# Seven block products instead of eight in the second MLP product of a hybrid decoder layer

## The chip, the cores and the metric

The kernel runs on one core of one Trainium2 chip, as one launch. The metric is device time in microseconds (us); the kernel before takes 1138.74 us (median of 3 runs, 1137.78 to 1138.87). TensorE (PE) multiplies matrices; PEld is its weight load, which overlaps the products. VectorE (DVE), ScalarE (ACT) and GpSimd (POOL) do element-wise work, and SyncE's queue (SP) issues nearly all DMAs.

## The reference

One layer (DEPTH = 1) over T = 272 tokens (16 learned meta tokens ahead of 256), width 2048, all in float32:

```
h = h + rmsnorm(mix, g_post_mix[l])
hn = rmsnorm(h, g_pre_ffn[l])
ff = jnp.square(jax.nn.relu(hn @ mlp_w1[l])) @ mlp_w2[l]
h = h + rmsnorm(ff, g_post_ffn[l])
return h[:, N_META:]
```

`mix` is the product of four mixers (S5, mLSTM, FoX attention, pooling) with `w_out`. `mlp_w1` is 2048 x 8192 and `mlp_w2` is 8192 x 2048. The change lies in the last product, of a 256 x 8192 activation with `mlp_w2` (the kernel works on the 256 tokens that are returned).

## The kernel before, in words

Every large weight is streamed from memory once, in jobs of 1 MB: a stage tile `wst` of 128 x 2048 (3 buffers) is loaded by one DMA. A job has two halves of 128 x 1024. `do_split` makes of each half two tiles in the PE's fp32r format: `wh` is a rounded copy (ACT, line 138), `wl` the rest, `wst - wh` (DVE, line 139). A product of two fp32 operands is then three fp32r products: high x high, high x low and low x high. The tiles `wh` and `wl` have 4 buffers each. The activations are split the same way by `split_act`: `ah` (ACT, line 173) and `al` (DVE, line 174), 128 x 256 for each channel tile, 4 buffers.

`stream` goes over all halves: before the products of half i are issued, the splits up to half i + 3 (`LOOK`) and the loads of the next two jobs have been issued. The order in which the instructions of one engine then stand is chosen by a planner, which works through the program by priority and by what its model finds ready; each engine runs its own queue strictly in that order.

The first MLP product (`up`, lines 1172 and 1173) leaves its result, channels on the partitions, in `H` and `Y`: 64 channel tiles of 128 channels x 256 tokens. The second product is two calls of `row_jobs` (line 223), one for each 1024 of the 2048 output columns. A job holds two channel tiles, a pair, of `mlp_w2`; there are 32 pairs in a call and 64 in all. For each channel tile, 2 token tiles of 128 and 2 column blocks of 512 make 4 accumulators of 128 x 512, each in a PSUM bank (tags `a0` to `a3` in the first call, `m0` to `m3` in the second), with three matmuls each: 24 matmuls of 128x128 by 128x512 for a pair. The last 2 (first call) or 4 (second call) channel tiles are held back and run accumulator by accumulator, so that `evac_a` and `evac_b` (square sums on ACT, line 1192; gain on DVE, lines 1201 and 1212; the residual and the output at the end, lines 1219 to 1223) can start on the first accumulators while PE works on the others.

`XC` (128 x 16 x 2 x 272 in fp32r) holds the split input of the first product and is not read any more once that is done.

Of the kernel before, what the change touches and what calls it, by code (L numbers as in the profile page):

```python
# [29 lines left out]
TH = T // 2  # L33
NK = D // P
DFF = 8192
NF = DFF // P
# [9 lines left out]
TILES = ((0, 16), (16, 128), (144, 128))  # L46
LOOK = 3
PACE = 2.0


def build(tc, A, out):
# [10 lines left out]
class Body:  # L62
# [41 lines left out]
    def need(self, *names):  # L104
        while not all(n in self.ready for n in names):
            yield 0
# [13 lines left out]
    def stream(self):  # L120
        nc = self.nc
        jobs = self.jobs
        halves = [(j, h) for j in jobs for h in range(2)]
        split = {}

        def do_split(i):
            j, h = halves[i]
            src = j["stage"][:, h * 1024:(h + 1) * 1024]
            if j.get("early"):
                wh = self.sb(self.post, [P, 1024], f"wh{j['early']}{h}", F32R)  # L130
                wl = self.sb(self.post, [P, 1024], f"wl{j['early']}{h}", F32R)
            else:
                wh = self.sb(self.wsp, [P, 1024], "wh", F32R)
                wl = self.sb(self.wsp, [P, 1024], "wl", F32R)
            n = 512 if i == 0 else 1024
            for a in range(0, 1024, n):
                cs = slice(a, a + n)
                nc.scalar.copy(wh[:, cs], src[:, cs])  # L138
                nc.vector.tensor_tensor(out=wl[:, cs], in0=src[:, cs], in1=wh[:, cs].bitcast(F32), op=ALU.subtract)  # L139
            split[i] = (wh, wl)  # L140
            if j.get("pre"):
                j["pre"](h)

        done = 0
        early = [i for i, (j, h) in enumerate(halves) if j.get("early")]
        for i, (j, h) in enumerate(halves):
            self.load(i // 2 + 3)
            if i == early[0] - 2:
                self.load(early[-1] // 2 + 1)
            while done < i + LOOK + 1 and done < len(halves) and (done not in early or i >= early[0] - 2):  # L150
                with ExitStack() as es:
                    if early[-1] < done <= early[-1] + LOOK + 1:
                        for ins in self.after:
                            es.enter_context(self.tc.issue_after(ins))
                    do_split(done)
# [12 lines left out]
    def split_act(self, src):  # L168

        nc = self.nc  # L170
        ah = self.sb(self.asp, [P, S], "ah", F32R, bufs=4)
        al = self.sb(self.asp, [P, S], "al", F32R, bufs=4)
        nc.scalar.copy(ah, src)  # L173
        nc.vector.tensor_tensor(out=al, in0=src, in1=ah.bitcast(F32), op=ALU.subtract)
        return ah, al


    def seg_jobs(self, name, w, c0, nk, xh, xl, t0, nt, evac, tags):
# [29 lines left out]
    def row_jobs(self, w, nk, act, need, c0, tags, lead, evac):  # L208

        nc = self.nc
        acc = {}
        sp = {}
        held = []

        def one(tok, c, k, w2):
            if (tok, c) not in acc:  # L220
                acc[tok, c] = self.bank(tags[2 * tok + c])
            for a, b in ((0, 0), (0, 1), (1, 0)):
                ins = nc.tensor.matmul(acc[tok, c], sp[k][a][:, tok * P:(tok + 1) * P], w2[b][:, c * 512:(c + 1) * 512],  # L223
                                       start=(k == 0 and (a, b) == (0, 0)), stop=(k == nk - 1 and (a, b) == (1, 0)))
            return ins.ins

        def job(k0):
            def pre(h):
                k = k0 + h
                if need:  # L230
                    self.drain(need(k))
                sp[k] = self.split_act(act(k))

            def mm(h, wh, wl):
                k = k0 + h
                if k < nk - lead:
                    for tok in range(2):
                        for c in range(2):
                            one(tok, c, k, (wh, wl))
                    return  # L240
                held.append((k, (wh, wl)))
                if k == nk - 1:
                    last = None
                    for tok in range(2):
                        for c in range(2):
                            with self.tc.issue_after(last) if last else nullcontext():
                                for kk, ww in held:
                                    ins = one(tok, c, kk, ww)
                            last = ins
                            with self.tc.high_priority():  # L250
                                evac(tok, c, acc[tok, c])
            return {"src": w[:, k0:k0 + 2, c0:c0 + 1024], "a": 2, "pre": pre, "mm": mm}

        return [job(k0) for k0 in range(0, nk, 2)]

    def rstd(self, ss, n, width, rows=P):

# [805 lines left out]
    def out_jobs(self):  # L1063
        nc, A = self.nc, self.A
        w = A["w_out"].rearrange("(k p) c -> p k c", p=P)
        act = lambda k: self.Y[:, k, :]
        st = {}

        def square(tok, c, acc):
# [82 lines left out]
    def ffn_jobs(self):  # L1152
# [1 line left out]
        w1 = A["mlp_w1"].rearrange("(k p) c -> p k c", p=P)  # L1154
        w2 = A["mlp_w2"].rearrange("(k p) c -> p k c", p=P)

        act = lambda f: self.H[:, f, :] if f < NF - NK else self.Y[:, f - (NF - NK), :]

        def up(g):
            tags = [f"{'ma'[g % 2]}{b}" for b in range(4)]  # L1160
            state = {}

            def mm_for(k0):
                def mm(h, wh, wl):
                    for b in range(4):
                        if b not in state:
                            state[b] = self.bank(tags[b])
                        acc = state[b]
                        for kk in range(2):
                            k = k0 + 2 * h + kk  # L1170
                            ws = slice(kk * 512 + b * P, kk * 512 + (b + 1) * P)
                            nc.tensor.matmul(acc.rearrange("p (a b) -> p a b", a=2), wh[:, ws], XC[:, k, :, 0:S], start=(k == 0), stop=False)  # L1172
                            nc.tensor.matmul(acc[:, 0:S], wl[:, ws], XC[:, k, 0, 0:S], start=False, stop=(k == NK - 1))  # L1173
                        if k0 + 2 * h + 2 == NK:
                            lo = z = self.sb(self.fp, [P, S], "lo", bufs=3)
                            nc.scalar.copy(lo, acc[:, S:2 * S])
                            nc.vector.tensor_tensor(out=z, in0=acc[:, 0:S], in1=lo, op=ALU.add)
                            nc.vector.scalar_tensor_tensor(out=z, in0=z, scalar=0.0, in1=self.rb2, op0=ALU.max, op1=ALU.mult)
                            nc.scalar.activation(act(4 * g + b), z, AF.Square)
                return mm  # L1180

# [7 lines left out]
        st = {}  # L1189
# [4 lines left out]
        def evac_a(tok, c, acc):  # L1194
            if (tok, c) == (0, 0):
                st["ss"] = self.sb(self.fp, [P, 2, 5], "fss")
                nc.gpsimd.memset(st["ss"][:, :, 4:5], EPS)
                st["m"] = self.sb(self.fp, [P, 2, 2, 512], "fm")
                st["gp"] = self.gain(self.fp, "g_post_ffn", 0)
            square(tok, c, acc)  # L1200
            nc.vector.tensor_tensor(out=st["m"][:, tok, c, :], in0=acc, in1=st["gp"][:, c * 512:(c + 1) * 512], op=ALU.mult)
            if (tok, c) == (1, 1):
                st["gp"] = self.gain(self.fp, "g_post_ffn", 1)

        def evac_b(tok, c, acc):
            X = self.X
            square(tok, 2 + c, acc)
            if c == 1:
                r = self.sb(self.fp, [P, 1], f"fr{tok}")
                self.rms(r, st["ss"][:, tok, :])  # L1210
            f = st[c] = self.sb(self.fp, [P, 512], "fin", bufs=2)
            nc.vector.tensor_tensor(out=f, in0=acc, in1=st["gp"][:, c * 512:(c + 1) * 512], op=ALU.mult)
            if c == 0:
                return
# [7 lines left out]
                    nc.vector.scalar_tensor_tensor(out=X[:, tok, cs], in0=m, scalar=r, in1=X[:, tok, cs], op0=ALU.mult, op1=ALU.add)  # L1222
                (nc.scalar if cc == 0 else nc.sync).dma_start(self.out[tok * P:(tok + 1) * P, cs], X[:, tok, cs])

        jobs += self.row_jobs(w2, NF, act, None, 0, ["a0", "a1", "a2", "a3"], 2, evac_a)
        jobs += self.row_jobs(w2, NF, act, None, 1024, ["m0", "m1", "m2", "m3"], 4, evac_b)
        return jobs


# [24 lines left out]
```

## Time and profile before

| | |
|---|---|
| median of 3 runs | 1138.74 us |
| time of the profiled execution | 1138.89 us |
| its span | 1136.9 us |
| PE busy | 1109.5 us (98%) |
| DVE busy | 717.2 us (63%) |
| ACT busy | 570.0 us (50%) |
| POOL busy | 196.1 us (17%) |
| mean DMA rate | 179 GB/s |

Busy time is the time in which at least one instruction of the engine was running. An instruction's duration in the profile can include a wait inside it, for instance for a port; its start can lie a little ahead of the end of the one before it on the same engine. Matmuls are pipelined: one of 128x512 shows 0.39 us, and the next starts well before that is over, so the pace is read from a stretch and its count. The second MLP product runs from about 780 us to 1128 us.

### The profile page before, as it was taken

The page shows a single profiled execution, that of the slowest core. Times are in us where ns is not written, and L with a number is a line of the kernel's source. Part 1 is how long each engine was busy: PE and PEld are TensorE (multiplying, and loading weights), DVE is VectorE, ACT ScalarE, POOL GpSimd, SP SyncE. Part 2 cuts the span into 40 slices and gives each one's busy share as a digit, 9 for nine tenths or more (in the row PEclk, how much of TensorE's full clock was granted, in tenths as well). Part 3 has the DMA queues.
Part 4 walks back from the last instruction along what each step waited for, and adds up shares of the span by engine and source line. Part 5 has one row for each costly group of instructions (what it writes and reads, how often), then busy time and mean ns, then how long its engine had stood idle before and what let it go on. Part 6 is the DMA issues. An engine that isn't in the chain of part 4 may idle for free.

```text
span 1136.9 us, 16603 instructions
## 1 busy us (share of the span) xinstructions
PE 1109.5 (98%) x6425; PEld 959.8 (84%) x6425; DVE 717.2 (63%) x1042; ACT 570.0 (50%) x918; POOL 196.1 (17%) x266
## 2 busy tenths in 40 slices
PE   8998999999999999999999999999999999999996
PEld 7897887999988878888888888888888888888885
DVE  5589998545556676555555555655666666666565
ACT  5634335445645567455445444545545455454543
POOL 6948887002151010000000000000000000000001
PEclk9999999999999999999999999999999999999999
DMA  8734334535447655665656566665655666556652
GB/s 252 214 96 155 112 112 137 175 126 175 152 131 261 214 172 179 199 191 186 190 186 185 186 185 189 186 191 172 222 190 185 192 202 217 186 189 197 203 189 74
DMA packets 91822, 203.31 MB, mean 179 GB/s; under 512 B 12996, under 2 KB 16192, under 8 KB 91488
## 3 DMA queue, kind: packets, MB, share of 16 engines
q1 hardware_dynamic: 90800, 201.45, 55.4%
q8 instruction: 50, 0.82, 0.3%
q10 hardware_dynamic: 848, 0.79, 0.2%
q14 instruction: 28, 0.23, 0.1%
q0 software_dynamic: 96, 0.02, 0.0%
HBM read 199.58 MB, written 2.11 MB: 177 GB/s over the span
## 4 chain that ended last, share of the span: by engine, by line
PE 83%; DVE 6%; POOL 3%; issue 1%; SPq 0%; ACT 0%; DMA 0%; DVEq 0%; POOLq 0%; ACTq 0%
PE a L223 19%; PE m L223 19%; PE m L1172 10%; PE a L1172 10%; PE m L1173 5%; PE a L1173 5%; PE a L197 3%; PE a L196 3%; PE a L195 3%; DVE wl L139 2%; DVE cv L864 1%; POOL si L836 1%; DVE wr L824 0%; POOL sr L834 0%; SPq L775 0%
## 5 line engine op out<-in xcount | busy, mean ns | idle before, releaser
L139 DVE TENSOR_TENSOR wl<-wst,wh 128x1024 fp32r<-128x1024 f32 (+1 forms) x365 | 454.9, 1248 | 271.9 <-ACT wh L138 271.6
L138 ACT CAST wh<-wst 128x1024 fp32r<-128x1024 f32 (+1 forms) x365 | 380.9, 1046 | 253.1 <-PE a L1172 85.3
L1172 PE MATMUL m<-xc,wh 128*128 128x512 f32 x512 | 179.9, 394 | 0.1
L1172 PE MATMUL a<-xc,wh 128*128 128x512 f32 x512 | 179.4, 394 | 0.0
L195 PE MATMUL a<-xc,wh 128*128 128x272 f32 (+2 forms) x576 | 168.3, 296 | 0.9 <-ACT wh L138 0.9
L196 PE MATMUL a<-xc,wh 128*128 128x272 f32 (+2 forms) x576 | 167.8, 293 | 0.0
L197 PE MATMUL a<-xc,wl 128*128 128x272 f32 (+2 forms) x576 | 166.9, 293 | 0.0
L1173 PE MATMUL m<-xc,wl 128*128 128x256 f32 x512 | 143.4, 280 | 0.0
L1173 PE MATMUL a<-xc,wl 128*128 128x256 f32 x512 | 143.0, 280 | 0.0
L223 PE MATMUL m<-wl,ah 128*128 128x512 f32 x320 | 124.6, 389 | 0.2 <-DVE wl L139 0.2
L223 PE MATMUL a<-wl,ah 128*128 128x512 f32 x320 | 124.7, 390 | 0.0
L223 PE MATMUL a<-wh,al 128*128 128x512 f32 x320 | 124.7, 390 | 0.0
L223 PE MATMUL m<-wh,al 128*128 128x512 f32 x320 | 124.5, 389 | 0.0
L223 PE MATMUL m<-wh,ah 128*128 128x512 f32 x320 | 123.2, 389 | 0.0
L223 PE MATMUL a<-wh,ah 128*128 128x512 f32 x320 | 123.1, 391 | 0.0
L367 POOL TENSOR_TENSOR fr<-fr,mhalf 128x1 f32<-128x1 f32 x2 | 1.1, 558 | 688.6 <-DVE fr L366 688.6
L1172 PEld LDWEIGHTS m<-xc,wh 128*128 128x128 f32 x512 | 96.1, 188 | 23.0 <-DVE xc L1132 0.3
L1172 PEld LDWEIGHTS a<-xc,wh 128*128 128x128 f32 x512 | 96.0, 188 | 22.8
L195 PEld LDWEIGHTS a<-xc,wh 128*128 128x128 f32 x576 | 109.3, 191 | 3.6 <-ACT wh L138 1.3
L196 PEld LDWEIGHTS a<-xc,wh 128*128 128x128 f32 x576 | 110.3, 192 | 1.4 <-issue 0.4
L197 PEld LDWEIGHTS a<-xc,wl 128*128 128x128 f32 x576 | 109.4, 191 | 1.7 <-issue 0.9
L173 ACT CAST ah<-h 128x256 fp32r<-128x256 f32 x96 | 38.9, 407 | 118.8 <-PE a L223 60.3
(310 smaller groups left out, 1442.7 us busy)
## 6 DMA issues: line engine op xcount, KB each, us to landing
wst<-in_mlp_w SPq DMA_DIRECT2D x128, 1024.0 KB, 5.2
wst<-in_w_in SPq DMA_DIRECT2D x34, 1024.0 KB, 5.1
wst<-in_w_out SPq DMA_DIRECT2D x16, 1024.0 KB, 5.2
x<-in_x SPq DMA_DIRECT2D x8, 256.0 KB, 3.5
wst<-in_ssm_glu_w SPq DMA_DIRECT2D x2, 1024.0 KB, 5.0
res<-in_x SPq DMA_DIRECT2D x1, 2048.0 KB
wst<-in_w_in SPq DMA_DIRECT2D x3, 512.0 KB, 8.5
out<-res SPq DMA_DIRECT2D x6, 256.0 KB, 2.4
```

Of the source, the lines that this page charges most:

```text
L138: nc.scalar.copy(wh[:, cs], src[:, cs])
L139: nc.vector.tensor_tensor(out=wl[:, cs], in0=src[:, cs], in1=wh[:, cs].bitcast(F32), op=ALU.subtract)
L173: nc.scalar.copy(ah, src)
L195: nc.tensor.matmul(acc[:, :nt], sh, xh(k, t0, nt), start=(k == 0), stop=False)
L196: nc.tensor.matmul(acc[:, :nt], sh, xl(k, t0, nt), start=False, stop=False)
L197: nc.tensor.matmul(acc[:, :nt], sl, xh(k, t0, nt), start=False, stop=(k == nk - 1))
L223: ins = nc.tensor.matmul(acc[tok, c], sp[k][a][:, tok * P:(tok + 1) * P], w2[b][:, c * 512:(c + 1) * 512], start=(k == 0 and (a, b) == (0, ...
L367: nc.gpsimd.tensor_tensor(out=dst, in0=dst, in1=self.mhalf[:, :dst.shape[1]], op=ALU.pow)
L836: g.tensor_tensor(out=si, in0=wr[:, ps], in1=sin[:, ps], op=ALU.mult)
L864: v.scalar_tensor_tensor(out=c, in0=x(tap), scalar=w(tap), in1=c, op0=ALU.mult, op1=ALU.add)
L1172: nc.tensor.matmul(acc.rearrange("p (a b) -> p a b", a=2), wh[:, ws], XC[:, k, :, 0:S], start=(k == 0), stop=False)
L1173: nc.tensor.matmul(acc[:, 0:S], wl[:, ws], XC[:, k, 0, 0:S], start=False, stop=(k == NK - 1))
```

## The change

29 of the 64 pairs go another way. `KINDS` says which: in the first call two plain pairs (N) and then 15 times S, N; in the second two plain ones, 14 times S, N, and two plain ones. A plain pair is computed as before (`plain`). For an S pair, the two channel tiles, the two token tiles and the two column blocks are taken as a 2 x 2 block product in Winograd's form of Strassen's: 7 block products of sums (`seven`), each three matmuls, 21 in all. The sums are made by POOL: four 128 x 512 differences of weight blocks, in place in the stage tile, and four 128 x 128 sums of activation blocks (tile `sums`). ACT and DVE split the plain weight blocks B11, B22 and B21 (1536 columns, into `whR`, `wlR`) ahead of the differences, and after them the four differences (2048 columns, into `whT`, `wlT`) and the four activation sums (512 columns, into `ahS`, `alS`). All these are single buffers, cut from `XC`. Four of the products (M1, M5, M6, M7) have accumulators of their own in the four PSUM banks that the call does not use; after the call's last S pair they are combined into four SBUF tiles (one ACT copy, four DVE adds), and at the end each plain accumulator gets its part added (one more DVE instruction) before `evac_a` or `evac_b`.

`split_act` now splits a pair's activations at once (128 x 512, 2 buffers instead of 4 of 128 x 256), with the second half of a job; `row_jobs`, which the product with `w_out` still uses, does so too. The tile `lo` of the first product has 2 buffers instead of 3, and `fin` is gone.

```diff
+KINDS = ("NN" + "SN" * 15, "NN" + "SN" * 14 + "NN")
...
         def do_split(i):
             j, h = halves[i]
+            if j.get("split"):
+                split[i] = j["split"](h, j["stage"])
+                return
...
-        ah = self.sb(self.asp, [P, S], "ah", F32R, bufs=4)
-        al = self.sb(self.asp, [P, S], "al", F32R, bufs=4)
+        ah = self.sb(self.asp, [P, 2 * S], "ah", F32R, bufs=2)
+        al = self.sb(self.asp, [P, 2 * S], "al", F32R, bufs=2)
...
+        whR, wlR, whT, wlT = cut(0, 1536), cut(1536, 1536), cut(3072, 2048), cut(5120, 2048)
+        ahS, alS = cut(7168, 512), cut(7680, 512)
...
+        def three(dst, ah, al, wh, wl, stop):
...
+            nc.tensor.matmul(b, ah, wh, start=first, stop=False)
+            nc.tensor.matmul(b, ah, wl, start=False, stop=False)
+            return nc.tensor.matmul(b, al, wh, start=False, stop=stop).ins
...
+                            with self.tc.high_priority():
+                                v = acc["part"][2 * tok + c]
+                                nc.vector.tensor_tensor(out=v, in0=acc[tok, c], in1=v, op=ALU.add)
+                                evac(tok, c, v)
...
+            def split(h, st):
+                b12, b11, b22, b21 = (st[:, i * 512:(i + 1) * 512] for i in range(4))
+                def hl(wh, wl, src):
+                    nc.scalar.copy(wh, src)
+                    nc.vector.tensor_tensor(out=wl, in0=src, in1=wh.bitcast(F32), op=ALU.subtract)
+                sub = lambda eng, o, a, b: eng.tensor_tensor(out=o, in0=a, in1=b, op=ALU.subtract)
+                if h == 0:
+                    hl(whR[:, 0:512], wlR[:, 0:512], b11)
+                    hl(whR[:, 512:1536], wlR[:, 512:1536], st[:, 1024:2048])
+                    return None, None
+
+                sub(nc.gpsimd, b11, b12, b11)
+                sub(nc.gpsimd, b12, b12, b22)
+                sub(nc.gpsimd, b22, b22, b11)
+                sub(nc.gpsimd, b21, b21, b22)
+                a = act(k0)
+                a11, a21, a12, a22 = (a[:, i * P:(i + 1) * P] for i in range(4))
+                sums = self.sb(self.fp, [P, 512], "sums")
+                s3, s2, s1, s4 = (sums[:, i * P:(i + 1) * P] for i in range(4))
+                sp[k0], sp[k0 + 1] = self.split_act(a)
+                sub(nc.gpsimd, s3, a21, a11)
+                nc.gpsimd.tensor_tensor(out=s1, in0=a21, in1=a22, op=ALU.add)
+                sub(nc.gpsimd, s2, s1, a11)
+                sub(nc.gpsimd, s4, a12, s2)
+                hl(ahS, alS, sums)
+                hl(whT[:, 0:1024], wlT[:, 0:1024], st[:, 0:1024])
+                hl(whT[:, 1024:2048], wlT[:, 1024:2048], st[:, 1024:2048])
+                return None, None
...
+                todo = ((("M1", "A11", "B11"), ((0, 1), "A12", "B21"), ((0, 0), "S4", "B22")),
+                        (("M5", "S1", "T1"), ("M7", "S3", "T3"), ("M6", "S2", "T2"), ((1, 1), "A22", "T4")))[h]
+                for dst, x, y in todo:
+                    three(dst, *A[x], *B[y], final and dst[0] == "M")
+                if h == 1 and final:
+                    add = lambda o, a, b: nc.vector.tensor_tensor(out=o, in0=a, in1=b, op=ALU.add)
+                    with self.tc.high_priority():
+                        c12, c11, c22, c21 = acc["part"] = part()
+                        nc.scalar.copy(c11, acc["M1"])
+                        add(c21, acc["M6"], c11)
+                        add(c12, acc["M5"], c21)
+                        add(c21, acc["M7"], c21)
+                        add(c22, acc["M5"], c21)
...
-                            lo = z = self.sb(self.fp, [P, S], "lo", bufs=3)
+                            lo = z = self.sb(self.fp, [P, S], "lo", bufs=2)
...
-        jobs += self.row_jobs(w2, NF, act, None, 0, ["a0", "a1", "a2", "a3"], 2, evac_a)
-        jobs += self.row_jobs(w2, NF, act, None, 1024, ["m0", "m1", "m2", "m3"], 4, evac_b)
+        ta, tm = ["a0", "a1", "a2", "a3"], ["m0", "m1", "m2", "m3"]
+        jobs += self.fast_jobs(w2, NF, act2, 0, tm, ta, KINDS[0], 2, part_a, evac_a)
+        jobs += self.fast_jobs(w2, NF, act2, 1024, ta, tm, KINDS[1], 4, part_b, evac_b)
```

## Rows read from the trace of the kernel before

**Rows 1.** Engines by busy time (share of the span), instructions: the page's first part.
```profile
PE 1109.5 (98%) x6425; PEld 959.8 (84%) x6425; DVE 717.2 (63%) x1042; ACT 570.0 (50%) x918; POOL 196.1 (17%) x266
```

**Rows 2.** Busy time by stretch: us, engines (instructions), granted clock, DMA share, GB/s.
```profile
780.00:953.00 173.00, 173.00 (x765) 143.24 (x764) 105.85 (x133) 88.06 (x135) 0.00 (x0) 1.00 0.59 191
954.00:1117.00 163.00, 163.00 (x721) 134.97 (x720) 100.79 (x123) 82.76 (x124) 0.00 (x0) 1.00 0.58 187
```

**Rows 3.** Last part of the chain that ended last: start, us, what.
```profile
779.60 174.19 PE a L223 x768
953.79 162.99 PE m L223 x719
```

**Rows 4.** Waits in 780 to 1117 us: waiter and releaser, total us, times, longest.
```profile
ACT ah L173 <- PE a L223: 82.1, 59, 4.3
ACT ah L173 <- PE m L223: 80.2, 59, 1.4
```

**Rows 5.** ACT and DVE groups by shape, 780 to 1117 us: busy, mean ns.
```profile
L138 ACT CAST wh<-wst 128x1024 fp32r<-128x1024 f32 x124 | 129.8, 1046 | 0.2 <-PE a L1172 0.2
L173 ACT CAST ah<-h 128x256 fp32r<-128x256 f32 x92 | 37.4, 407 | 118.8 <-PE a L223 60.3 <-PE m L223 58.5
...
L139 DVE TENSOR_TENSOR wl<-wst,wh 128x1024 fp32r<-128x1024 f32 x124 | 151.9, 1225 | 61.0 <-ACT wh L138 61.0
L174 DVE TENSOR_TENSOR al<-h,ah 128x256 fp32r<-128x256 f32 x92 | 39.1, 425 | 50.1 <-ACT ah L173 50.0
```

**Rows 6.** The split's two lines, whole span: min/median/max ns (the 128x512 form is the shortest).
```profile
L138 ACT CAST wh<-wst x365: 618/1048/1062, 7.0 to 1117.1; 128x1024 fp32r<-128x1024 f32 x182, 128x512 fp32r<-128x512 f32 x1
L139 DVE TENSOR_TENSOR wl<-wst,wh x365: 685/1226/2387, 7.7 to 1118.2; 128x1024 fp32r<-128x1024 f32 x182, 128x512 fp32r<-128x512 f32 x1
```

**Rows 7.** POOL tensor_tensor of 128x512 (mean) and of 128x128 (min/median/max).
```profile
L974 POOL TENSOR_TENSOR keyrow<-keyrow,trimask 128x512 f32<-128x512 f32 x2 | 2.6, 1294 | 2.7 <-DMA keyrow<-grows 2.7
L836 POOL TENSOR_TENSOR si<-wr,sin x16: 446/526/1446, 101.0 to 183.8; 128x128 f32<-128x128 f32 x16
```

**Rows 8.** POOL and DVE side by side at 84 to 89 us: start, us, instruction.
```profile
84.70 1.55 POOL L754 TENSOR_TENSOR sin<-sin,cos 128x544 f32<-128x544 f32 x1
86.21 2.08 POOL L753 TENSOR_TENSOR cos<-tok,s5col 128x544 f32<-128x544 f32 x1
...
84.96 2.38 DVE L139 TENSOR_TENSOR wl<-wst,wh 128x1024 fp32r<-128x1024 f32 x1
```

**Rows 9.** The same at 1130 to 1133 us, 128x512 on both engines.
```profile
1130.68 0.74 DVE L1222 SCALAR_TENSOR_TENSOR res<-fin,fr,res 128x512 f32<-128x512 f32 x1
...
1130.81 1.74 POOL L1220 TENSOR_TENSOR res<-res,fm 128x512 f32<-128x512 f32 x1 [0.83 <-ACT fm L1219]
...
1131.34 1.75 DVE L1222 SCALAR_TENSOR_TENSOR res<-fin,fr,res 128x512 f32<-128x512 f32 x1
```

**Rows 10.** The same at 107 to 111 us, 128x128 on POOL.
```profile
107.11 1.41 DVE L139 TENSOR_TENSOR wl<-wst,wh 128x1024 fp32r<-128x1024 f32 x1
109.51 1.36 DVE L139 TENSOR_TENSOR wl<-wst,wh 128x1024 fp32r<-128x1024 f32 x1
...
107.40 1.44 POOL L836 TENSOR_TENSOR si<-wr,sin 128x128 f32<-128x128 f32 x1
109.87 1.32 POOL L833 TENSOR_TENSOR pm<-wi,sin 128x128 f32<-128x128 f32 x1
```

**Rows 11.** Busy time by stretch (columns as in rows 2) about an early pause of PE.
```profile
93.00:96.60 3.60, 0.12 (x2) 0.00 (x0) 3.60 (x7) 0.66 (x1) 3.60 (x3) 1.00 0.67 258
97.70:101.10 3.40, 3.40 (x18) 3.40 (x18) 3.40 (x7) 3.40 (x7) 1.61 (x3) 0.50 0.00 1
```

**Rows 12.** DVE's gain on a last accumulator, from PSUM, in the kernel's tail.
```profile
1129.27 0.68 DVE L1212 TENSOR_TENSOR fin<-m,gp 128x512 f32<-128x512 f32 x1
```

**Rows 13.** DMA of the MLP weights: issues, KB each, median us to landing.
```profile
wst<-in_mlp_w SPq DMA_DIRECT2D x128, 1024.0 KB, 5.2
```

More of the change, by code (lines that the diff above doesn't have):

```diff
@@ L170, in split_act @@
         nc = self.nc
-        ah = self.sb(self.asp, [P, S], "ah", F32R, bufs=4)
-        al = self.sb(self.asp, [P, S], "al", F32R, bufs=4)
+        ah = self.sb(self.asp, [P, 2 * S], "ah", F32R, bufs=2)
+        al = self.sb(self.asp, [P, 2 * S], "al", F32R, bufs=2)
         nc.scalar.copy(ah, src)
         nc.vector.tensor_tensor(out=al, in0=src, in1=ah.bitcast(F32), op=ALU.subtract)
-        return ah, al
+        return [tuple(t[:, i * S:(i + 1) * S] for t in (ah, al)) for i in range(2)]
     def seg_jobs(self, name, w, c0, nk, xh, xl, t0, nt, evac, tags):
@@ L228, in pre @@
             def pre(h):
-                k = k0 + h
+                if h == 0:
+                    return
                 if need:
-                    self.drain(need(k))
-                sp[k] = self.split_act(act(k))
+                    self.drain(need(k0), need(k0 + 1))
+                sp[k0], sp[k0 + 1] = self.split_act(act(k0))
             def mm(h, wh, wl):
@@ L254, in row_jobs, with fast_jobs, one, plain @@
         return [job(k0) for k0 in range(0, nk, 2)]
+    def fast_jobs(self, w, nk, act, c0, tags, tags7, kinds, lead, part, evac):
+        nc = self.nc
+        free = self.XC.rearrange("p a b c -> p (a b c)")
+        cut = lambda a, n: free[:, a:a + n]
+        whR, wlR, whT, wlT = cut(0, 1536), cut(1536, 1536), cut(3072, 2048), cut(5120, 2048)
+        ahS, alS = cut(7168, 512), cut(7680, 512)
+        acc = {}
+        sp = {}
+        held = []
+        last_s = max(i for i, kd in enumerate(kinds) if kd == "S")
+        tagof = {(t, c): tags[2 * t + c] for t in range(2) for c in range(2)}
+        tagof.update({f"M{m}": tags7[i] for i, m in enumerate((1, 5, 6, 7))})
+        def three(dst, ah, al, wh, wl, stop):
+            first = dst not in acc
+            if first:
+                acc[dst] = self.bank(tagof[dst])
+            b = acc[dst]
+            nc.tensor.matmul(b, ah, wh, start=first, stop=False)
+            nc.tensor.matmul(b, ah, wl, start=False, stop=False)
+            return nc.tensor.matmul(b, al, wh, start=False, stop=stop).ins
+        def one(tok, c, k, w2):
+            ah, al = sp[k]
+            ts, cs = slice(tok * P, (tok + 1) * P), slice(c * 512, (c + 1) * 512)
+            return three((tok, c), ah[:, ts], al[:, ts], w2[0][:, cs], w2[1][:, cs], k == nk - 1)
+        def plain(k0):
+            def pre(h):
+                if h == 1:
+                    sp[k0], sp[k0 + 1] = self.split_act(act(k0))
+            def mm(h, wh, wl):
+                k = k0 + h
+                if k < nk - lead:
+                    for tok in range(2):
+                        for c in range(2):
+                            one(tok, c, k, (wh, wl))
+                    return
+                held.append((k, (wh, wl)))
+                if k == nk - 1:
+                    last = None
+                    for tok in range(2):
+                        for c in range(2):
+                            with self.tc.issue_after(last) if last else nullcontext():
+                                for kk, ww in held:
+                                    ins = one(tok, c, kk, ww)
+                            last = ins
+                            with self.tc.high_priority():
+                                v = acc["part"][2 * tok + c]
+                                nc.vector.tensor_tensor(out=v, in0=acc[tok, c], in1=v, op=ALU.add)
+                                evac(tok, c, v)
+            return pre, mm
+        def seven(k0, final):
+            def split(h, st):
[4 more added lines that the diff above has]
+                sub = lambda eng, o, a, b: eng.tensor_tensor(out=o, in0=a, in1=b, op=ALU.subtract)
+                if h == 0:
+                    hl(whR[:, 0:512], wlR[:, 0:512], b11)
[18 more added lines that the diff above has]
+                return None, None
+            def mm(h, wh, wl):
+                A = {}
+                for kk, (n0, n1) in enumerate((("A11", "A21"), ("A12", "A22"))):
+                    for i, n in enumerate((n0, n1)):
+                        A[n] = tuple(t[:, i * P:(i + 1) * P] for t in sp[k0 + kk])
+                for i, n in enumerate(("S3", "S2", "S1", "S4")):
+                    A[n] = tuple(t[:, i * P:(i + 1) * P] for t in (ahS, alS))
+                B = {n: (whR[:, i * 512:(i + 1) * 512], wlR[:, i * 512:(i + 1) * 512]) for i, n in enumerate(("B11", "B22", "B21"))}
+                B.update({n: (whT[:, i * 512:(i + 1) * 512], wlT[:, i * 512:(i + 1) * 512]) for i, n in enumerate(("T3", "T1", "T2", "T4"))})
+                todo = ((("M1", "A11", "B11"), ((0, 1), "A12", "B21"), ((0, 0), "S4", "B22")),
[11 more added lines that the diff above has]
+                        add(c22, acc["M5"], c21)
+            return split, mm
+        jobs = []
+        for i, kd in enumerate(kinds):
+            j = {"src": w[:, 2 * i:2 * i + 2, c0:c0 + 1024], "a": 2}
+            if kd == "S":
+                j["split"], j["mm"] = seven(2 * i, i == last_s)
+            else:
+                j["pre"], j["mm"] = plain(2 * i)
+            jobs.append(j)
+        return jobs
@@ L1065, in out_jobs @@
         w = A["w_out"].rearrange("(k p) c -> p k c", p=P)
-        act = lambda k: self.Y[:, k, :]
+        act = lambda k: self.Y[:, k:k + 2, :].rearrange("p a b -> p (a b)")
         st = {}
@@ L1155, in ffn_jobs, with act @@
         w2 = A["mlp_w2"].rearrange("(k p) c -> p k c", p=P)
-        act = lambda f: self.H[:, f, :] if f < NF - NK else self.Y[:, f - (NF - NK), :]
+        def act(f, n=1):
+            t, f = (self.H, f) if f < NF - NK else (self.Y, f - (NF - NK))
+            return t[:, f:f + n, :].rearrange("p a b -> p (a b)")
+        act2 = lambda f: act(f, 2)
         def up(g):
@@ L1197, in evac_a @@
                 nc.gpsimd.memset(st["ss"][:, :, 4:5], EPS)
-                st["m"] = self.sb(self.fp, [P, 2, 2, 512], "fm")
                 st["gp"] = self.gain(self.fp, "g_post_ffn", 0)
             square(tok, c, acc)
-            nc.vector.tensor_tensor(out=st["m"][:, tok, c, :], in0=acc, in1=st["gp"][:, c * 512:(c + 1) * 512], op=ALU.mult)
+            nc.vector.tensor_tensor(out=acc, in0=acc, in1=st["gp"][:, c * 512:(c + 1) * 512], op=ALU.mult)
             if (tok, c) == (1, 1):
@@ L1210, in evac_b @@
                 self.rms(r, st["ss"][:, tok, :])
-            f = st[c] = self.sb(self.fp, [P, 512], "fin", bufs=2)
+            f = st[c] = acc
             nc.vector.tensor_tensor(out=f, in0=acc, in1=st["gp"][:, c * 512:(c + 1) * 512], op=ALU.mult)
@@ L1223, in evac_b, with part_a, part_b @@
                 (nc.scalar if cc == 0 else nc.sync).dma_start(self.out[tok * P:(tok + 1) * P, cs], X[:, tok, cs])
-        jobs += self.row_jobs(w2, NF, act, None, 0, ["a0", "a1", "a2", "a3"], 2, evac_a)
-        jobs += self.row_jobs(w2, NF, act, None, 1024, ["m0", "m1", "m2", "m3"], 4, evac_b)
+        def part_a():
+            st["m"] = self.sb(self.fp, [P, 2, 2, 512], "fm")
+            return [st["m"][:, tok, c, :] for tok in range(2) for c in range(2)]
+        def part_b():
+            return [self.H[:, 2 * i:2 * i + 2, :].rearrange("p a b -> p (a b)") for i in range(4)]
+        ta, tm = ["a0", "a1", "a2", "a3"], ["m0", "m1", "m2", "m3"]
+        jobs += self.fast_jobs(w2, NF, act2, 0, tm, ta, KINDS[0], 2, part_a, evac_a)
+        jobs += self.fast_jobs(w2, NF, act2, 1024, ta, tm, KINDS[1], 4, part_b, evac_b)
         return jobs
```

## The prediction

> **What bounds the kernel now.** I read the engines' shares first: PE is busy for 98% of the span, DVE for 63%, ACT for 50%, POOL for 17% [rows 1]. Shares of the whole say little about one stage, so the next view is the busy time by stretch. In the second MLP product (780 to 1117 us) PE is busy in all of 173 and 163 us, DVE in 61% of them, POOL in none; the granted clock is 1.00, the upper of its two levels, 2.4 GHz [rows 2]. The chain that ended last agrees: from 779.60 us on it is one piece of PE for 174.19 us and 768 matmuls [rows 3], so a matmul goes by every 174.19 / 768 = 0.2268 us, though each shows a longer time. A pair of 24 takes 5.44 us, two pairs 10.89 us. The waits say the same from the other side: ACT waits for PE (82.1 and 80.2 us, for the buffers of `ah`), not PE for ACT or DVE [rows 4]. In this stage the time is PE's count of matmuls, and DVE, ACT and the DMA (5.2 us for a job [rows 13], with others in flight) keep up with it.
>
> **What it takes off PE.** An S pair has 21 matmuls instead of 24: 3 x 0.2268 = 0.68 us, for 29 pairs 19.7 us. That is the whole gain, and it comes only if the other engines prepare an S pair and the N pair behind it within PE's new time for both, 45 x 0.2268 = 10.21 us. So I work out one such period, S and N.
>
> **What it adds on ACT.** Casts: for S 512 + 1024 (plain blocks), 512 (activations), 512 (sums), 2 x 1024 (differences); for N 2 x 1024 and 512. With 1.05 us for 1024 [rows 5] and 0.62 us for 512 [rows 6], 5 x 1.05 + 4 x 0.62 = 7.73 us. That fits in 10.21.
>
> **What it adds on DVE and POOL.** DVE subtracts once for each cast. Taken singly, at 1.23 us for 1024 [rows 5] and 0.69 us for 512 [rows 6], 5 x 1.23 + 4 x 0.69 = 8.91 us: it would fit. POOL's four differences of 128x512 at 1.29 us and four sums of 128x128 at 0.45 us [rows 7] are 6.96 us: that fits too. But before, POOL stood still in this stage [rows 2], and the earlier stages show what the two do to each other. At 84.96 us DVE starts a `wl` while POOL runs until 84.70 + 1.55 = 86.25 us; it ends at 87.34 us, 1.09 us after POOL, and takes 2.38 us instead of 1.23. POOL's next one starts at 86.21 us and ends 0.95 us after DVE's end [rows 8]. At the end of the kernel, with 128x512 on both: POOL ends 1.13 us after DVE's end at 1131.42 us, and DVE's next one 0.54 us after POOL's end at 1132.55 us [rows 9]. For 128x128 on POOL it is twice 0.32 us after the end of `wl` [rows 10]. So a DVE instruction with two SBUF inputs and a POOL `tensor_tensor` don't run beside each other: the second one does its work when the first is over. Every `wl` and `al` of the change is of that kind, and so are all eight of POOL's.
>
> So the two need one thing in turn, and their times in it add up. For a period, DVE 5 x 1.09 + 4 x 0.54 = 7.61 us, POOL 4 x 1.13 + 4 x 0.32 = 5.80 us, together 13.41 us. That is more than PE's 10.21 and more than the 10.89 of two pairs before. The stage turns from PE-bound to bound by what DVE and POOL share, and the price is at least 29 x (13.41 - 10.89) = 73.1 us.
>
> The Trainium skill, "SBUF — State Buffer", section "SBUF: two separate sides", says that GpSimd and a VectorE instruction with two SBUF inputs take a pair of ports in turn, each for its whole instruction. The trace agrees that they exclude each other, but POOL's 128x512 needs only 1.13 us [rows 9] of its 1.29 us [rows 7] once DVE lets go, so I count what the rows show and keep the whole instructions as a rival.
>
> **What waits add.** The floor is reached only if one of the two always has something ready. The upper bound comes from the order in which the code is written. `whR`, `whT` and `ahS` exist once, POOL's differences overwrite the stage after its plain blocks have been split, and ACT and DVE stand in their queues behind the sums. Walk from the end of DVE's first subtraction (B11) to the same one of the next S pair, with the durations above: second subtraction 1.09, first difference 1.13, `al` 0.54, second difference 1.13, third and fourth alone 2 x 1.29, four sums alone 4 x 0.45, then ACT's cast of the sums 0.62 and of the first differences 1.05 with nothing on DVE but the sums' subtraction, DVE's two subtractions of differences 2.18, two of N 2.18, `al` of N 0.54, the next B11 0.54: 15.4 us, or 29 x 4.47 = 130 us more. The planner needn't keep that order: POOL's four sums need no weights and can go ahead of the differences, and the splits of N can stand beside POOL. I take 14.0 us, 0.6 above the floor and 1.4 below the walk, because those two moves are open and would fill most of the gaps: 29 x (14.0 - 10.89) = 90.2 us.
>
> **The rest of the edits.** The tail gets one DVE add ahead of the last square and gain, 0.68 us by the gain's own row [rows 12]; those of the first three accumulators lie beside PE. The two combinations (one ACT copy, four adds, about 0.6 + 4 x 0.68 = 3.3 us) lie beside the pair behind them; uncovered 6.6 us. Joined splits of activations save ACT 2 x 0.41 - 0.62 = 0.20 us a pair [rows 5, 6], off the path. They come a half later: before, `ah` waited for PE by 82.1 + 80.2 us in 118 times without PE waiting in turn [rows 4]; they now stand two halves, 5.4 us, ahead of their product instead of three, and cost 0; uncovered it is a half, 2.7 us, at each call's start. Two `lo` instead of three hold ACT up at the end of each of the 16 column groups, under the three halves of weights split ahead: 0; a wait of one DVE instruction there, uncovered, is 16 x 0.4 = 7 us. The DMA has more time than before.
>
> **The sum.** Against the profiled execution (1138.89 us, span 1136.9 and 2.0 around it, 0.15 above the median): 1138.9 + 90.2 + 0.7 = 1229.8 us, say 1230. With floor and walk, 1212.7 to 1269.
>
> **Rivals.** *PE stays the bound.* If POOL's work lay beside DVE's, the engines would need 10.21 (PE), 8.91 and 6.96 us, and with the sums ahead of the differences PE could run on: 1138.9 - 19.7 + 0.7 = 1120 us. For it: each engine alone fits, and PE is the bound today. Against it: rows 8 to 10, where nothing runs beside. It decides from the point where DVE and POOL together need less than 10.21 us of what they share; they need 13.41. 5%.
>
> *Each holds what they share for its whole instruction*, as in two POOL instructions with a DVE one between them that cannot use POOL's start. Then the period is 8.91 + 6.96 = 15.87 us: 1138.9 + 29 x 4.98 + 0.7 = 1284 us. For it: rows 8 to 10 show exclusion. Against it: the 1.13 us of 1.29 above. It is the rule of the page named above. 8%.
>
> *The two do not exclude each other here, but the written order holds.* Then from B11 to B11: POOL 6.96, the casts 0.62 and 1.05, DVE 2.18 + 2.18 + 0.54 + 0.54, 14.1 us: 1138.9 + 29 x 3.2 + 0.7 = 1232 us, the forecast's time by another cause; with half of POOL's chain filled it is 10.6 us, and 1131 us. Same objection. 6%, a third of it faster or within 0.2%.
>
> *The queues interlock.* If the planner's order differs from what the chip has ready, PE's products come into the ring too, since `whR`, `whT` and `ahS` may only be rewritten once PE has read them. With one PE half (12 matmuls, 2.72 us) in series: 15.4 + 2.7 = 18.1 us, 1138.9 + 29 x 7.2 + 0.7 = 1348 us. For it: all S buffers are single. PE would also pause: at 93.0 to 96.6 us it worked 0.12 us of 3.6, and at 97.7 to 101.1 us the granted clock was 0.50, the lower level, 1.2 GHz [rows 11]. PE has 13.4 - 10.2 = 3.2 us to spare in a period, and 3.4 us at half the clock cost it 1.7, so that alone does not set the period. Against it: the splits of N have four buffers and need nothing from S. 9%.
>
> That the change doesn't do what it says is excluded by its count, 21 `three` matmuls for an S pair.
>
> **How the numbers follow.** The forecast (bound by what DVE and POOL share, 1213 to 1269 us) has 72%, the rivals 5, 8, 6 and 9. The range must hold 8 in 10: from 1197 us, which lets 16 us of the floor's 73 be hidden beside the six N pairs that stand outside the alternation or by holds shorter than read, to 1285 us, the time of the second rival. Within 0.2% (2.3 us) is about what a measurement of this kernel can't tell from no change. Faster: the first rival and one of the third's 6 points, 0.06; same: 0.01; slower: 0.93.
>
> **What would show it.** Right: in the second product PE busy 70 to 75% instead of 100%, a period of 13.4 to 15.4 us, `wl` of the S pairs' stretch well over 1.23 us on average, POOL's differences over 1.29 us, DVE and POOL nearly without a common idle moment, and PE's idle time ended by DVE's `wl`. The first rival: PE still 100% and `wl` at 1.23 us. The second: a period near 15.9 us with no common idle moment of DVE and POOL. The third: PE pauses, but `wl` stays at 1.23 us beside POOL. The fourth: DVE and POOL both idle for long, waiting for PE. The forecast is wrong if the period is below 13 us, or if the time is lost outside 780 us to the end.

## The result, and the profile after

The changed kernel takes 1226.12 us (median of 4 runs, 1225.55 to 1227.52) against 1138.61 us for the kernel before (median of 4 runs), a ratio of 1.0772 with a 95% interval of 1.0753 to 1.0790: 87.5 us slower, forecast 1230.

First the page's engine line, which answers to [rows 1].

```profile
PE 1133.3 (93%) x6338; PEld 955.1 (78%) x6338; DVE 885.2 (72%) x1065; ACT 616.0 (50%) x927; POOL 541.7 (44%) x498
```

PE issued fewer matmuls and the span grew to 1224.5 us. The busy time by stretch says where. Its columns are those of [rows 2]; the first line is the end of the first MLP product in the kernel before, the second the same in the changed kernel, and the others are the first call of the second product, the step from one call to the next, and the second call.

```profile
447.00:779.00 332.00, 332.00 (x1899) 289.39 (x1899) 184.37 (x236) 161.86 (x236) 0.00 (x0) 1.00 0.61 188
...
447.00:779.00 332.00, 332.00 (x1899) 291.03 (x1898) 186.02 (x237) 161.34 (x237) 3.89 (x5) 1.00 0.61 188
...
790.00:1000.00 210.00, 176.33 (x684) 129.32 (x682) 184.51 (x142) 109.02 (x141) 174.34 (x119) 0.95 0.46 157
1000.00:1025.00 25.00, 23.94 (x98) 19.39 (x99) 23.40 (x26) 12.87 (x22) 9.24 (x7) 0.93 0.55 186
1025.00:1195.00 170.00, 142.23 (x553) 108.24 (x552) 149.20 (x111) 90.67 (x113) 148.24 (x97) 0.93 0.45 149
```

From 447 to 779 us PE has lost nothing: 1899 matmuls in 332 us, as before. In the first call PE ran 684 matmuls in 210 us; at the pace of before (0.2268 us each) that is 155 us of work, 74%. DVE is busy in 88% and POOL in 83% of the same stretch. From first cast to first cast, the S pairs of the first call follow one another every 14.02 us on average, those of the second every 14.35. But these means hold the first spacing of each call, 22.6 and 24.5 us. After the start the spacings settle: in the first call 16.0 and 11.3 us in turn, in the second 16.7 and 10.6, in both 27.3 us for two, so 13.65 us for one. Three S pairs of the first call begin with these casts on ACT:

```profile
879.33 1.57 ACT L329 CAST xc<-wst 128x512 fp32r<-128x512 f32 x2
...
890.66 0.61 ACT L329 CAST xc<-wst 128x512 fp32r<-128x512 f32 x1
...
906.64 1.56 ACT L329 CAST xc<-wst 128x512 fp32r<-128x512 f32 x2
```

In the first call DVE and POOL are both idle in only 2% of the time.

The waits from 790 to 1200 us (waiter, releaser, total us, times, longest) have turned round against [rows 4]: now PE and its weight load wait for DVE and ACT, ACT for POOL, and POOL for DVE.

```profile
ACT xc L329 <- POOL wst L331: 137.5, 48, 5.6
DVE xc L330 <- ACT xc L329: 37.8, 31, 2.3
POOL wst L331 <- DVE xc L330: 34.6, 16, 10.4
...
PEld m L290 <- DVE xc L330: 28.1, 8, 4.2
PE m L290 <- DVE xc L330: 24.3, 8, 3.7
```

In the groups by shape of the same stretch, against [rows 5, 7], the same instructions have become longer: `wl` of 128x1024 from 1225 to 1661 ns, POOL's 128x512 from 1294 to 1938, its 128x128 from a median of 526 (446 at the least) to means of 892 to 1285, by the tiles it reads. ACT's cast of 128x1024 is unchanged (1046 and 1048).

```profile
L331 POOL TENSOR_TENSOR wst<-wst 128x512 f32<-128x512 f32 x112 | 217.1, 1938 | 40.0 <-DVE xc L330 34.6
L330 DVE TENSOR_TENSOR xc<-wst,xc 128x1024 fp32r<-128x1024 f32 x85 | 130.6, 1548 | 36.5 <-ACT xc L329 36.5
L146 DVE TENSOR_TENSOR wl<-wst,wh 128x1024 fp32r<-128x1024 f32 x63 | 102.7, 1661 | 7.8 <-ACT wh L145 7.8
L329 ACT CAST xc<-wst 128x1024 fp32r<-128x1024 f32 x84 | 87.5, 1048 | 138.2 <-POOL wst L331 137.5
...
L331 POOL TENSOR_TENSOR sums<-sums,h 128x128 f32<-128x128 f32 x21 | 27.0, 1285 | 0.9
```

One handover inside an S pair, from the timelines of DVE and POOL (start, us):

```profile
901.27 1.32 DVE L330 TENSOR_TENSOR xc<-wst,xc 128x1024 fp32r<-128x1024 f32 x1 [2.24 <-ACT xc L329]
...
901.59 2.16 POOL L331 TENSOR_TENSOR wst<-wst 128x512 f32<-128x512 f32 x1
...
902.52 1.78 DVE L330 TENSOR_TENSOR xc<-sums,xc 128x512 fp32r<-128x512 f32 x1
```

POOL starts at 901.59 while DVE runs until 902.59, and ends at 903.75, 1.16 us after it; DVE's next one starts at 902.52 and ends at 904.30, 0.55 us after POOL. These are the 1.13 and 0.54 us of [rows 9]. The chain that ended last, from 880 to 910 us, is that alternation: of its 30 us 55% are POOL's instructions, 35% DVE's, and none is a matmul.

```profile
by line: POOL wst L331 40.2%; DVE wl L146 19.2%; DVE xc L330 13.8%; POOL sums L331 12.0%; issue 8.8%; ACT xc L329 3.5%; POOL sums L347 2.9%; DVE al L181 2.0%; DVEq L181 0.1%; POOLq L331 0.1%
```

### The profile page after: what moved, and what is told of

It reads as the page before. It is cut to its first block, busy times and chain, and to the rows that moved or that the text cites. A ratio compares the mean times of both kernels' runs of the same rounds, so it can differ in the third digit from the quotient of the medians.

```text
span 1224.5 us, 16618 instructions
## 1 busy us (share of the span) xinstructions
PE 1133.3 (93%) x6338; PEld 955.1 (78%) x6338; DVE 885.2 (72%) x1065; ACT 616.0 (50%) x927; POOL 541.7 (44%) x498
## 4 chain that ended last, share of the span: by engine, by line
PE 54%; POOL 21%; DVE 15%; issue 5%; ACT 3%; DMA 2%; DVEq 0%; POOLq 0%; SPq 0%; ACTq 0%
POOL wst L331 12%; PE m L1309 10%; PE a L1309 10%; DVE wl L146 6%; PE m L1310 5%; PE a L1310 5%; PE a L204 4%; PE a L203 4%; PE a L202 4%; DVE xc L330 4%; PE a L231 4%; PE m L231 3%; POOL sums L331 3%; ACT xc L329 2%; DMA wst<-in_mlp_w 1%
## 5 line engine op out<-in xcount | busy, mean ns | idle before, releaser
L146 DVE TENSOR_TENSOR wl<-wst,wh 128x1024 fp32r<-128x1024 f32 (+1 forms) x307 | 412.1, 1352 | 225.9 <-ACT wh L145 225.7
L145 ACT CAST wh<-wst 128x1024 fp32r<-128x1024 f32 (+1 forms) x307 | 317.3, 1044 | 283.7 <-PE a L1309 86.8
L331 POOL TENSOR_TENSOR wst<-wst 128x512 f32<-128x512 f32 x116 | 225.0, 1940 | 347.2 <-DVE xc L330 341.6
L330 DVE TENSOR_TENSOR xc<-wst,xc 128x1024 fp32r<-128x1024 f32 (+1 forms) x116 | 155.4, 1367 | 37.0 <-ACT xc L329 37.0
L329 ACT CAST xc<-wst 128x1024 fp32r<-128x1024 f32 (+1 forms) x116 | 106.2, 940 | 145.8 <-POOL wst L331 139.6
L204 PEld LDWEIGHTS a<-xc,wl 128*128 128x128 f32 x576 | 110.0, 192 | 1.8 <-issue 1.1
L1310 PEld LDWEIGHTS m<-xc,wl 128*128 128x128 f32 x512 | 96.7, 189 | 0.0
L1310 PEld LDWEIGHTS a<-xc,wl 128*128 128x128 f32 x512 | 96.5, 188 | 0.0
L289 PE MATMUL a<-wh,ah 128*128 128x512 f32 x144 | 59.2, 416 | 1.8 <-ACT ah L180 1.8
L290 PE MATMUL a<-wl,ah 128*128 128x512 f32 x144 | 58.3, 407 | 1.3 <-DVE wl L146 1.3
L289 PE MATMUL m<-wh,ah 128*128 128x512 f32 x136 | 55.8, 410 | 0.0
```

Of the source, the lines that this page charges most:

```text
L204: nc.tensor.matmul(acc[:, :nt], sl, xh(k, t0, nt), start=False, stop=(k == nk - 1))
L289: nc.tensor.matmul(b, ah, wh, start=first, stop=False)
L329: nc.scalar.copy(wh, src)
L330: nc.vector.tensor_tensor(out=wl, in0=src, in1=wh.bitcast(F32), op=ALU.subtract)
L331: sub = lambda eng, o, a, b: eng.tensor_tensor(out=o, in0=a, in1=b, op=ALU.subtract)
```

## The experiments

Theory: DVE instructions with two SBUF inputs and POOL's `tensor_tensor`, which reads SBUF, run in turn, so their times add up and set the period. First rival: the ring of single buffers and queue order, with POOL's length in it, sets it. Ratios are against the kernel before, with 95% intervals.

**x1_memset.** POOL has as much work as its differences and sums take alone, but reads nothing.

```diff
-                sub(nc.gpsimd, b11, b12, b11)
...
+                for t in (b11, b12, b22, b21):
+                    for _ in range(3):
+                        nc.gpsimd.memset(t, 0.5)
...
+                for t in (s3, s1, s2, s4):
+                    nc.gpsimd.memset(t, 0.5)
```

> The 29 S pairs as in the changed kernel, but POOL reads nothing: each 128x512 difference is replaced by three memsets of its block and each 128x128 sum by one memset (12 x 0.52 + 4 x 0.20 = 7.0 us of POOL in an S pair, as long as its differences and sums alone); the values are left out. Theory (DVE and POOL take something in turn that POOL's two-input instruction needs): a memset does not hold DVE up, wl of 128x1024 stays at 1.23 us, the period is near PE's 10.2 us, 1120 to 1140 us. Rival (the ring of single buffers and queue order, with POOL's length in it, sets the period): POOL is as long as before, so the time stays at 1210 to 1230 us.

1134.52 us, 0.996 (0.9945 to 0.9975). From 800 to 1100 us, by shape:

```profile
L339 POOL MEMSET wst<- 128x512 f32 x324 | 159.3, 529 | 120.9 <-DVE xc L330 77.3 <-DMA wst<-in_mlp_w 29.1 <-DVE wl L146 9.2
L330 DVE TENSOR_TENSOR xc<-wst,xc 128x1024 fp32r<-128x1024 f32 x82 | 99.4, 1222 | 38.9 <-ACT xc L329 38.7
L146 DVE TENSOR_TENSOR wl<-wst,wh 128x1024 fp32r<-128x1024 f32 x58 | 69.0, 1221 | 14.6 <-ACT wh L145 14.6
```

DVE is back at 1.22 us and 91.6 of the changed kernel's 1226.1 us are gone, with POOL's own work kept as long. Two other things differ: the planner's order, since it takes other lengths for POOL, and a memset need not wait for a value that it would have read. x7 and x8 are all but free of the first: of DVE's 326 instructions from 700 us on, one stands elsewhere.

**x2_nopool.** POOL's work left out altogether.

```diff
-                sub(nc.gpsimd, b11, b12, b11)
...
-                hl(ahS, alS, sums)
+                hl(ahS, alS, a)
```

> POOL's differences and sums are left out (the blocks themselves are split again in their place, so ACT, DVE and PE have the same instructions). Theory: DVE alone needs at most 8.9 us in a period, so PE's 10.2 us bound again and the whole gain shows, 1138.7 - 19.7 + 0.7 = 1120 us (1117 to 1126). Rival (the seven products cost PE more than their count, by the accumulators' alternation or by the waits of single buffers): above 1135 us though POOL does nothing.

1120.97 us, 0.9842 (0.9825 to 0.9858). From 800 to 1100 us PE is at its pace of before, 1322 matmuls in 300 us:

```profile
800.00:1100.00 300.00, 299.57 (x1322) 247.72 (x1321) 248.48 (x272) 206.25 (x266) 0.00 (x0) 1.00 0.62 198
```

The seven products do bring their whole 19.7 us when nothing holds up their inputs: the last matmul ends at 1108.6 us, 1128.4 before. The 13.5 us between x1 and x2 are what is left without exclusion, by the length of POOL's chain or by the other order; the two were not told apart. After the first spacing, the S pairs of the first call come every 10.5 us in x1 and every 10.2 us in x2, which is PE's own time for them.

**x3_dve.** Differences and sums on DVE.

```diff
-                sub(nc.gpsimd, b11, b12, b11)
+                sub(nc.vector, b11, b12, b11)
...
-                sub(nc.gpsimd, s4, a12, s2)
+                sub(nc.vector, s4, a12, s2)
```

> All differences and sums move from POOL to DVE, so nothing is taken in turn, but DVE gets 4 x 0.60 + 4 x 0.22 = 3.3 us more in a period, 8.1 + 3.3 = 11.4 us from start to start. Theory: DVE is the bound, 1138.7 + 29 x (11.4 - 10.9) + 0.7 = 1154 us (1140 to 1175). Rival (the ring of single buffers sets the period): the same chain with shorter links, 12.5 us by the walk, 1186 us.

1173.14 us, 1.0290 (1.0273 to 1.0307): 53 us faster than with POOL beside it, at the upper end of what the theory gave. In the first call the period is 12.47 us with the first spacing of 18.3 us, and 12.02 us without it. DVE is busy in 95.5% of the latter, 11.5 us where 11.4 had been counted, and waits add 0.5 us. DVE bounds, but the rival's 12.5 us is as near, so this run alone decides nothing.

**x4_quarter.** 15 S pairs instead of 29.

```diff
-KINDS = ("NN" + "SN" * 15, "NN" + "SN" * 14 + "NN")
+KINDS = ("NN" + "SNNN" * 7 + "SN", "NN" + "SNNN" * 7 + "NN")
```

> Only every fourth pair goes through the seven products (15 of 64, S N N N), with POOL as in the changed kernel. Theory: in a period of four pairs DVE and POOL need 13.41 + 2 x 2.72 = 18.9 us of what they share, PE 93 x 0.2268 = 21.1 us, so PE bounds: 1138.7 - 15 x 0.68 + 0.7 = 1129 us (1126 to 1136), faster than the kernel before. Rival (each S pair costs its own ring of waits, 3.0 us as in the changed kernel): 1138.7 + 15 x 3.0 = 1184 us.

1176.62 us, 1.0326 (1.0311 to 1.0342): the theory's number is missed by 48 us, though four pairs leave 2.2 us to spare; the rival's 1184 us, a ring of waits in each S pair, is missed by 7. The timelines of ACT and DVE show one S pair. Its first cast is at 895.46 us and its last subtraction ends at 910.95, 15.5 us later, which is also the median of the 15.

```profile
895.46 1.57 ACT L329 CAST xc<-wst 128x512 fp32r<-128x512 f32 x2 [4.57 <-DMA wst<-in_mlp_w]
...
900.45 1.04 ACT L329 CAST xc<-wst 128x1024 fp32r<-128x1024 f32 x1 [2.38 <-POOL wst L331]
...
897.07 2.20 DVE L330 TENSOR_TENSOR xc<-wst,xc 128x1024 fp32r<-128x1024 f32 x1 [0.26 <-ACT xc L329]
899.19 1.77 DVE L330 TENSOR_TENSOR xc<-sums,xc 128x512 fp32r<-128x512 f32 x1
...
909.72 1.23 DVE L330 TENSOR_TENSOR xc<-wst,xc 128x1024 fp32r<-128x1024 f32 x1 [2.26 <-ACT xc L329]
```

A sum over four pairs was the wrong measure: the S pair's work can't start before its stage has landed, and then comes in one burst, in which the engines still take turns.

**x5_quarter_memset.** The edits of x4 and x1 together.

> The kernel with 15 of 64 pairs (every fourth), with POOL's differences and sums replaced by memsets as long as they are (values left out). It tells apart why 15 S pairs lost about 3.2 us each though DVE and POOL have time enough in four pairs. Theory (turn-taking inside the S pair itself makes it late): without it PE bounds, 1126 to 1135 us. Rival (the stage tile is held long by POOL's chain, so the next loads and S pairs are late): POOL's chain is as long as before, 1160 to 1180 us.

1132.90 us, 0.9943 (0.9929 to 0.9958). POOL's own work is as long (6.8 us from its first memset to its last; its differences in x4 are spread over 11.7 us), and ACT waits for the stage's DMA as much (52.1 us in 13 times from 800 to 1100 us; 55.2 in 13 in x4). But an S pair is now ready 9.1 us after its first cast instead of 15.5, and PE is busy in 298 of 300 us. So it is not the loads that cost 44 us in x4 but, for the most part, the turns inside the burst; POOL also starts 1.4 us earlier here, since its first memset waits for no split, and the order differs. Why 15.5 us are too long for PE is not shown: in x6 below, an S pair takes 14.2 us (median, 11.4 to 23.2) and PE loses little.

**x6_quarter_dve.** The edits of x4 and x3 together.

> 15 of 64 pairs through the seven products, with differences and sums on DVE: POOL stands still. DVE's need in four pairs is 8.1 + 3.3 + 2 x 2.9 = 17.2 us, PE's 21.1. Theory (nothing is taken in turn, and DVE has room): 1129 us (1126 to 1136), faster than the kernel before. Rival (the stage tile is held while the differences are made, 9 us instead of 13, and the loads behind it come late): 1145 to 1165 us.

1132.80 us, 0.9940 (0.9923 to 0.9957): 0.6% faster than the kernel before, and faster than the changed one. POOL is idle, `wl` takes 1218 ns, and PE is busy in 298.5 of 300 us.

**x7_before_pool.** The kernel before, with POOL work that nothing waits for but the stage's release.

```diff
                 sp[k] = self.split_act(act(k))
+                if not need:
+                    s = jj[0]["stage"]
+                    for q in range(PQ[h]):
+                        o = s[:, h * 1024:h * 1024 + 512]
+                        nc.gpsimd.tensor_tensor(out=o, in0=o, in1=s[:, h * 1024 + 512:(h + 1) * 1024], op=ALU.subtract)
```

> The kernel before, and in the second product POOL makes two in-place 128x512 differences in the stage for each half, after its split; nobody reads them. PE, ACT and DVE have what they had. For a pair POOL needs 4 x 1.29 = 5.2 us alone, less than PE's 5.44. Theory: DVE and POOL together need 2 x 1.09 + 2 x 0.3 + 4 x 1.13 = 7.3 us of what they share, so the pair takes up to 7.3 us: 1200 to 1258 us, and wl of 128x1024 well over 1.23 us. Rival (no exclusion, the order of the S pairs is the cause): 1138 to 1145 us, wl at 1.23 us.

1262.53 us, 1.1081 (1.1065 to 1.1098). The stretch from 800 to 1100 us, its groups, and DVE's timeline:

```profile
800.00:1100.00 300.00, 246.19 (x983) 177.95 (x981) 300.00 (x168) 110.15 (x172) 295.00 (x165) 1.00 0.44 146
```

```profile
L240 POOL TENSOR_TENSOR wst<-wst 128x512 f32<-128x512 f32 x165 | 298.1, 1834 | 5.0 <-DVE wl L140 1.2
L140 DVE TENSOR_TENSOR wl<-wst,wh 128x1024 fp32r<-128x1024 f32 x82 | 188.8, 2303 | 0.0
```

```profile
899.96 2.31 DVE L140 TENSOR_TENSOR wl<-wst,wh 128x1024 fp32r<-128x1024 f32 x1
902.20 1.52 DVE L175 TENSOR_TENSOR al<-h,ah 128x256 fp32r<-128x256 f32 x1
903.63 2.31 DVE L140 TENSOR_TENSOR wl<-wst,wh 128x1024 fp32r<-128x1024 f32 x1
```

Both engines look fully busy, DVE 300.00 of 300 us, yet it got through 82 `wl` where x8 has 111. A half repeats every 903.63 - 899.96 = 3.67 us, a pair every 7.34 us: the 7.3 that the holds add up to, and 64 x (7.34 - 5.44) = 122 us in all, a little over the range given.

**x8_before_memset.** The same with memsets.

```diff
-PQ = (2, 2)
+PQ = (5, 5)
...
-                        nc.gpsimd.tensor_tensor(out=o, in0=o, in1=s[:, h * 1024 + 512:(h + 1) * 1024], op=ALU.subtract)
+                        nc.gpsimd.memset(o, 0.5)
```

> The same with five memsets of 128x512 for each half instead of two differences: POOL 10 x 0.52 = 5.2 us a pair, as long, and the stage held as long, but nothing is read. Theory: 1138 to 1145 us, wl at 1.23 us. Rival (any POOL work of this length in the stage holds up the loads or DVE): slower like the one with differences, over 1170 us.

1139.32 us, 1.0000 (0.9991 to 1.0009), with POOL busy for 278 of 300 us:

```profile
L240 POOL MEMSET wst<- 128x512 f32 x559 | 278.6, 529 | 21.8 <-DVE wl L140 4.5
L140 DVE TENSOR_TENSOR wl<-wst,wh 128x1024 fp32r<-128x1024 f32 x111 | 135.8, 1225 | 61.7 <-ACT wh L139 61.6
```

PE, ACT and DVE have the same work in x7 and x8, there is no S pair and no ring, and POOL is occupied nearly as long (295 and 278 of 300 us). So it is neither POOL's being busy nor its holding the stage that lengthens `wl`: the exclusion of `wl` and POOL's `tensor_tensor` is shown. That it is the reading of SBUF in which the two POOL instructions differ for DVE is the nearest explanation; no other reading instruction of POOL was tried.

**x9_third_dve and x10_two5_dve.** More S pairs, all on DVE (20 and 23 of 64).

```diff
+KINDS = ("NN" + "SNN" * 10, "NN" + "SNN" * 10)
...
+KINDS = ("NN" + "SNNSN" * 6, "NN" + "SNNSN" * 5 + "SNN" + "NN")
```

> 20 of 64 pairs (S N N) through the seven products, differences and sums on DVE. In three pairs DVE needs 8.1 + 3.3 + 2.9 = 14.3 us, PE 69 x 0.2268 = 15.65 us. Theory: PE bounds, 1138.8 - 20 x 0.68 + 0.7 = 1126 us, and with the 4 us that the version with 15 pairs lost beside its own sum, 1130 us (1125 to 1134). Rival (DVE's work for an S pair comes in a burst that the buffers do not spread over three pairs): 1138 to 1155 us.

> 23 of 64 pairs (S N N S N) through the seven products, differences and sums on DVE. In five pairs DVE needs 2 x 8.5 + 3 x 2.9 = 25.7 us, PE 2 x 4.76 + 3 x 5.44 = 25.9 us. Theory: DVE and PE are even, so the S pairs gain nothing more, and every wait shows: 1130 to 1145 us. Rival (PE still bounds): 1124 us.

1136.52 us, 0.9980 (0.9971 to 0.9989), and 1143.11 us, 1.0033 (1.0021 to 1.0045). x9 lies between the two theories. By stretch, PE runs at its full pace (0.2268 us for a matmul) but for the step from the first call to the second:

```profile
800.00:960.00 160.00, 160.00 (x706) 131.93 (x705) 146.47 (x207) 99.42 (x128) 0.00 (x0) 1.00 0.56 196
960.00:990.00 30.00, 26.10 (x100) 20.38 (x100) 25.36 (x36) 16.85 (x21) 0.00 (x0) 0.89 0.64 216
990.00:1100.00 110.00, 110.00 (x487) 91.06 (x486) 99.02 (x136) 66.02 (x81) 0.00 (x0) 1.00 0.55 192
```

From 960 to 990 us, 100 matmuls take 30 us instead of 22.7, by pauses and by the lower clock behind them. So PE does bound within the calls, and the loss lies at that step, not in every S pair. x10 is where it was expected. Of the versions in which all sums are made, x6 stays the fastest.

## Why the prediction was right, step by step

- **PE's gain.** 19.7 us was right in size: x2 shows 1121 us where 1138.7 - 19.7 + 0.7 = 1120 was the sum, and its last matmul ends 19.8 us earlier than before.
- **The shared resource.** The step that turned the sign was right: exclusion from the early stages' rows holds in the second product, with the same holds (1.16 and 0.55 us against 1.13 and 0.54), and x7 against x8 isolates it.
- **The period.** The forecast was 14.0 us between a floor of 13.4 and a walk of 15.4; the settled period is 13.65. The floor was computed and is right; the 0.6 us of waits on top was a choice, and 0.24 were found. That the means, 14.02 and 14.35, meet the forecast is luck, since they hold the long first spacings. So is part of the total: 29 x (13.65 - 10.89) = 80 us where 90.2 were counted. But the last matmul ends 85.7 us later than before, so another 5.7 us were lost outside the settled stretches, which the sum has at nothing. Where is not shown: the first spacings are long in x2 too, 16.9 and 22.4 us, and there PE loses nothing. Both grounds for the choice show in the timelines: POOL's queue has the sums ahead of the remaining differences, and the `wl` of N take turns with POOL's work.
- **Each holds for its whole instruction** (15.87 us, 1284 us) is out, with 13.65 us. By the Trainium skill, "SBUF — State Buffer", section "SBUF: two separate sides", the engine that starts first has the shared pair of ports for its whole instruction. Here the other engine waits until the end, as that says, but POOL's 128x512 then takes 1.16 us, not its whole 1.29.
- **PE stays the bound** fell with x1 and x2: it would have been 1121 us if POOL had cost nothing. The third rival (no exclusion, but the written order) fell with x7 and x8: `wl` takes 2.30 us beside POOL's differences and stays at 1.23 us beside memsets. The fourth (the queues interlock by way of PE) asked for DVE and POOL both idle for long; they are in 2% of the time. Order and POOL's length without exclusion cost no more than 13.5 us (x1 against x2).
- **The tail** was mis-sized: 0.7 us was forecast; from the last matmul (ends at 1214.1 us, 1128.4 before) to the end of the span it is 10.4 us instead of 8.5. The last two adds stand behind the first token tile's residuals on DVE and run together from 1214.14 us, after the last matmul:

```profile
1212.82 1.41 DVE L1358 SCALAR_TENSOR_TENSOR res<-h,fr,res 128x512 f32<-128x512 f32 x2
1214.14 1.28 DVE L321 TENSOR_TENSOR h<-a,h 128x512 f32<-128x512 f32 x2
```

- **What would show it**: PE's busy share was forecast at 70 to 75% and reads 84%; by count it is 74%. About half of the difference, 10 of 21 us, are the 42 matmuls at the lower clock (1.2 GHz), which took 19.8 us; the rest is not accounted for. PE's idle time is ended by DVE, but mostly by the S pair's `xc` (line 330), not by `wl`.

## What to carry to other kernels

An engine that stands idle in the bounding stage is not free: before moving work to it, look in the trace for stretches in which it ran beside the engines that the stage needs, and read how each one's durations change there. Two busy shares of 88% and 83% can be one resource that is hardly ever free; the sign is a duration longer than the same shape elsewhere that ends the same short time after the other engine's end. A budget that fits on average over a period says little if the work comes in a burst (x4: 18.9 of 21.1 us, and 3% slower than before). And a mean period is to be read without its first spacing: a start of 22.6 us hid that the settled period was 13.65 and not 14.0.

## What the runs showed of the hardware that was not expected

- POOL's memset of 128x512 (529 ns) does not hold up DVE at all, although it writes SBUF for 93% of the time in x8: `wl` 1225 ns, as without it. Only its `tensor_tensor`, which reads SBUF, did.
- PE's clock fell in the changed kernel: granted 0.95, 0.93 and 0.93 in the three stretches of the second product above, with 13 falls to the lower level (1.2 GHz) before the last matmul, 47.8 us in all, where the kernel before had none in that product. Ahead of each of them PE had paused for its inputs, for 1.9 us or more together. What that alone cost was not tried. It is not on the chain shown above, which has no matmul.
